# Hybrid encoder layer: q and k squared and normalised from PSUM, the softmax sum as a column of v, f16 halves for q and k

## The chip, the cores and the metric

The kernel runs on one core of one Trainium2 chip. The metric is the device time of one execution in microseconds, from the profile's first to last instruction for traces, and as measured by repeated runs for times. Lower is better. The core has five engines with a program of their own: PE (TensorE, matmul, with its weight loads shown as PEld), DVE (VectorE), ACT (ScalarE), POOL (GpSimd) and SP (SyncE, which here issues nearly all DMAs).

## The reference

Two sequences of 1024 positions and 1024 channels go through one encoder layer. What matters here is the attention half:

```python
h = rms_norm(x, norm1); proj = h @ w_in
q = rms_norm(q.reshape(B, S, N_KV, GROUP, HEAD_DIM), q_gain)   # 8 heads of 64
k = rms_norm(k.reshape(B, S, N_KV, HEAD_DIM), k_gain)          # 2 kv heads
scores = einsum(q, k of the three neighbouring blocks of 128) / sqrt(64)
scores = where(|rel| <= 128 and inside, scores + bias[bucket(rel), head], -1e30)
m = max(max(scores), sink)
e = exp(scores - m)
probs = e / (sum(e) + exp(sink - m))
out = probs @ v
```

Beside it stands a gated mixing branch (gu, gv, a 128 x 128 matrix per head). Both are normalised, concatenated, projected by w_o and added to x, and a SwiGLU FFN follows. Everything is float32 in the reference.

## The kernel before, in words

Float32 products are made of halves: every operand is split into a high and a low part (`split`, `split_gain`, L113 to L127, ACT for the high part, DVE for the rest), and a product is three matmuls, high times high, high times low, low times high (`mm3`, L224). In the attention stage the parts are f32r or, for v and the probabilities, f16. In the FFN they are f16.

The 2 x 1024 positions are 16 tiles of 128 rows. The kernel has these stages:

1. Start: x and w_q arrive by k-slices, the q products of tiles 0 to 3 run as data arrives (L246 to L258), then w_kv, the row statistics, and the bias. The bias is a row per head, `row_d` in DRAM, made by one matmul of the table with a one-hot matrix. It is loaded so that partition p holds the row shifted by p (`sh`, L290), and `bias_turn` (L294) multiplies by a reversing matrix on PE and copies the product to SBUF on DVE, eight times.
2. Attention, tile after tile, laid out by an event list. Each function is put at a time with `at(time, fn, ...)` (L562 to L639), times are `8 * t` for tile t plus offsets from the tables AT and TW (L46 to L66), and the list is sorted and emitted. These numbers are priorities and no microseconds: the tool that orders each engine's instructions moves a ready one forward where an earlier one would wait, so that the q and kv products of later tiles (`fill`) stand between the score groups of earlier ones.
3. Gating products, the output projection by seven products for two pairs of halves (a Strassen-like scheme), and the FFN in the same scheme, up to the end.

One tile of stage 2 passes through:

- `proj_pieces` (L325): 24 matmuls into a PSUM tile pq (512 columns), ACT scales them by the row's factor into SBUF `qk` (L335), then 24 matmuls into pkv (256 columns).
- `proj_evac` (L350): ACT scales k into `qk` (L353) and v's high half (L356), then squares the 640 columns of q and k into `sq` (L359).
- `qk_sum` (L361): DVE makes v's low half (L364) and the ten sums of squares (L368), and POOL raises them to the power -1/2 (L161).
- `qk_scale` (L371): DVE multiplies `qk` by the ten factors in place (L374).
- `qk_turn` (L376): PE transposes k into pk and q into pt, two PSUM tiles.
- `qk_hi` and `qk_lo` (L385, L392): ACT writes the high halves of k and q with their gains, DVE the low halves, all f32r.
- `Attn.scores` (L415), four times a tile, one call for a pair of heads (one of each kv head): six matmuls, three per head, the two heads on the upper and lower 64 rows of the array at once (L423). DVE adds the bias and takes the minimum of the negated scores in one operation with an accumulator (L428).
- `exps` (L439): ACT exponentiates with an accumulator that gives the softmax sum (L444).
- `turn` and `turn_dma` (L464, L472): the probabilities are split into f16 halves (ACT L468, DVE L469) and transposed by DMA into pT (L476).
- `pv` (L480): per head and key block three f16 matmuls of 64 columns (L489 to L491) into one PSUM tile po of all eight heads.
- `norm`, `norm2`, `finish`, `finish_pow`, `finish2` (L453 to L513): the sink's term, the reciprocal of the sums, the scaling of po (L495), its own norm, and the store.

PSUM has two pools of four banks: `mm` holds pq, pkv (from tile 4 on), pk, pt, po and the gating products; `xx` holds the scores, pkv of tiles 0 to 3 and small things. SBUF tiles of 4 KB a partition come from pools named by tag: "L" 12, "M" 8, "XL" 3, "XN" 3, "S" 9. L holds k's halves (two tiles a sequence), v's halves (one), part of pT, the outputs o, and later the gating matrices, parts of w_o, FFN operands and w_down.

Of the kernel before, what the change touches and what calls it, by code (L numbers as in the profile page):

```python
# [9 lines left out]
F32 = mybir.dt.float32  # L10
# [6 lines left out]
P = 128  # L17
# [24 lines left out]
W_NORM = 16384.0  # L42
A_NORM = 16384.0
# [3 lines left out]
    loadx=-43.881, xhi=-33.043, xlo=-30.276, rsum=-29.644, rpow=-29.313, proj=-23.505, pstep=0.544, evac=0.058, qksum=-15.892,  # L47
    scale=-12.631, turnq=-12.312, hi=-10.517, lo=-7.619, sc=0.192, tr=3.624, trd=4.116, pv=2.327, ex=2.811,
    norm=6.71, norm2=11.259, finish=17.507, finish_pow=17.97, finish2=40.676, gmf=-26.818, gmstep=2.858, ld_gv=-5.686, st1=1.728,
    ld_gu=21.124, sp_gv=-2.88, sp_gu=25.516, gvstep=0.02, gustep=0.288, bias=-3.338, biasstep=0.673, st2=11.369,  # L50
# [3 lines left out]
    mx0=-13.949, mx1=-11.679, xr0=-11.199, xr1=-7.545, ta=-5.743, tb=-3.638, tc=1.886, nu=8.268, nt=8.797, h0=10.459,  # L54
    p0=13, h1=14.83, p1=15.401, raw0=45.957, raw1=54.748, prep=52.704, preps=0.249, tl=57.369, tls=0.412, tk=58.051,
    tks=0.597, ul=64.811, uls=0.974, uk=67.481, uks=0.956,
)
TW = {
# [11 lines left out]
def kernel(  # L70
# [25 lines left out]
    slots = {"L": 12, "M": 8, "XL": 3, "XN": 3, "S": 9}  # L96
# [4 lines left out]
    def h16(name, shape=(P, KD, 512), dt=F32R):  # L101
        return big.tile(list(shape), dt, tag="h16", name=name)

# [42 lines left out]
    qgs, kgs = (cst[:, 3 * KD + 2 * NH + n : 3 * KD + 2 * NH + n + 1] for n in range(2))  # L146
    n2s = cp.tile([P, KD], F32, name="n2s")

    qg8 = cp.tile([P, 1], F32, name="qg8")
    nc.vector.tensor_scalar_mul(qg8, qgs, -1.0 / math.sqrt(HD))  # L150
# [52 lines left out]

    xms = {}

# [13 lines left out]
    def rstd1_pow(t):  # L219
        e = small("x_e", 1)  # L220
        nc.vector.tensor_scalar_add(e, xms.pop(t), EPS)
        nc.gpsimd.tensor_tensor(rstd1[t], e, nhalf[:, :1], ALU.pow)

# [22 lines left out]
    for k in range(KD):  # L246
# [16 lines left out]
        if k == 2:  # L263
            ps_row = xx("ps_row", [NH, 512])
            nc.tensor.matmul(ps_row, tabs, oh, start=True, stop=True)
            rows = k4("S", "rows", (NH, 512))
            nc.vector.tensor_scalar_mul(rows, ps_row, -1.0)
            nc.gpsimd.dma_start(row_d, rows)
# [4 lines left out]
    for t in range(GROUP):  # L273
        rstd1_load(t, "L")

    rev = k4("S", "rev", (P, P))
    nc.gpsimd.memset(rev, 0.0)
    nc.gpsimd.affine_select(
        out=rev,
        in_=rev,  # L280
        compare_op=ALU.not_equal,
        fill=1.0,
        base=1 - P,
        pattern=[[1, P]],
        channel_multiplier=1,
    )
    shifted = []
    for h in range(0, NH, 2):
        sh = k4("M", f"sh{h}", (P, 2, 384))
# [1254 lines left out]
```

## Time and profile before

| what | value |
|---|---|
| timed runs | 1838.2, 1835.81, 1833.97 us, median 1835.81 |
| profiled execution, span | 1834.5 us |
| instructions | 26027 |
| PE busy | 1809.8 us, 99% |
| DVE busy | 1161.2 us, 63% |
| ACT busy | 1005.3 us, 55% |
| POOL busy | 104.4 us, 6% |
| mean granted TensorE clock | 0.998 |

The profiled execution shows no time of its own beside its span; the timed runs are other executions of the same program. A group row of the profile reads: line, engine, operation, output <- inputs, shapes, count, then busy time in us and the mean of one in ns, then the idle time of the engine just before such instructions and what ended it. A timeline row reads: start in us, duration in us, engine, line, operation, and in brackets an idle time before it and what ended that. A row of the stretches' view reads: from and to, its length, busy time of each engine with the number of instructions, the granted TensorE clock, the busy share of the DMA engines, and GB/s. A row of waits reads: who waited, for whom, the total in us, how often, and the longest. Matmuls are pipelined, so that their durations overlap, and the distance from start to start tells the pace.

### The profile page before, as it was taken

The page shows a single profiled execution, that of the slowest core. Times are in us where ns is not written, and L with a number is a line of the kernel's source. Part 1 is how long each engine was busy: PE and PEld are TensorE (multiplying, and loading weights), DVE is VectorE, ACT ScalarE, POOL GpSimd, SP SyncE. Part 2 cuts the span into 40 slices and gives each one's busy share as a digit, 9 for nine tenths or more (in the row PEclk, how much of TensorE's full clock was granted, in tenths as well). Part 3 has the DMA queues.
Part 4 walks back from the last instruction along what each step waited for, and adds up shares of the span by engine and source line. Part 5 has one row for each costly group of instructions (what it writes and reads, how often), then busy time and mean ns, then how long its engine had stood idle before and what let it go on. Part 6 is the DMA issues. An engine that isn't in the chain of part 4 may idle for free.

```text
span 1834.5 us, 26027 instructions
## 1 busy us (share of the span) xinstructions
PE 1809.8 (99%) x9696; PEld 988.6 (54%) x9696; DVE 1161.2 (63%) x2191; ACT 1005.3 (55%) x1926; POOL 104.4 (6%) x139
## 2 busy tenths in 40 slices
PE   8999999999999999999999999999999999999999
PEld 7677767887555444444444444444444444444444
DVE  4988883657788796564564555645646946554751
ACT  6899997655677775453444534534534553333340
POOL 2212110101100000000000000000000000000000
PEclk9999999999999999999999999999999999999999
DMA  7798998433556774331322313313362754333641
GB/s 244 165 195 176 193 194 280 139 112 105 183 193 202 246 249 137 124 128 54 127 89 107 109 69 121 110 40 120 108 232 87 268 185 150 92 115 104 231 137 46
DMA packets 206427, 273.66 MB, mean 149 GB/s; under 512 B 102707, under 2 KB 129331, under 8 KB 206300
## 3 DMA queue, kind: packets, MB, share of 16 engines
q1 hardware_dynamic: 206124, 271.72, 48.2%
q8 instruction: 76, 1.25, 0.3%
q10 hardware_dynamic: 144, 0.26, 0.1%
q14 instruction: 51, 0.42, 0.1%
q0 software_dynamic: 32, 0.02, 0.0%
HBM read 172.84 MB, written 76.04 MB: 136 GB/s over the span
## 4 chain that ended last, share of the span: by engine, by line
PE 91%; DVE 3%; DMA 2%; ACT 2%; issue 1%; POOL 0%; SPq 0%; ACTq 0%; POOLq 0%; DVEq 0%
PE pd L1382 7%; PE pd L1383 7%; PE pd L1381 7%; PE pa L1119 4%; PE pa L1121 4%; PE pa L1120 4%; PE pd L1119 4%; PE pd L1121 4%; PE pd L1120 4%; PE pc L1120 4%; PE pc L1121 4%; PE pc L1119 4%; PE pb L1119 2%; PE pq L226 2%; PE pb L1120 2%; PE pb L1121 2%
## 5 line engine op out<-in xcount | busy, mean ns | idle before, releaser
L1383 PE MATMUL pd<-wop,a 128*128 128x512 f16 x616 | 233.5, 379 | 0.0
L1382 PE MATMUL pd<-wop,a 128*128 128x512 f16 x616 | 233.5, 379 | 0.0
L1381 PE MATMUL pd<-wop,a 128*128 128x512 f16 x616 | 233.5, 379 | 0.0
L1120 PEld LDWEIGHTS <-op 128*128 128x128 f16 x1232 | 120.6, 98 | 147.2 <-issue 5.4
L1119 PEld LDWEIGHTS <-op 128*128 128x128 f16 x1232 | 122.4, 99 | 142.9 <-issue 0.5
L1121 PEld LDWEIGHTS <-op 128*128 128x128 f16 x1232 | 120.7, 98 | 146.0 <-issue 1.1
L1119 PE MATMUL pa<-top,op 128*128 128x512 f16 x352 | 133.9, 380 | 2.0 <-ACT ua L1226 2.0
L1121 PE MATMUL pa<-top,op 128*128 128x512 f16 x352 | 134.1, 381 | 0.0
L1120 PE MATMUL pa<-top,op 128*128 128x512 f16 x352 | 133.9, 380 | 0.0
L126 ACT ACTIVATE wop<-wd,wdr_r 128x512 f16<-128x512 f32 x66 | 47.2, 719 | 151.6 <-PE pd L1383 149.0
L126 ACT ACTIVATE a<-as,asr_r 128x512 f16<-128x512 f32 x154 | 102.0, 709 | 33.3 <-DMA as<-act_d 13.0
L1237 ACT COPY ub<-pc 128x512 f32<-128x512 f32 x44 | 25.7, 585 | 159.6 <-PE pc L1121 159.6
L127 DVE SCALAR_TENSOR_TENSOR a<-as,asr_r,a 128x512 f16<-128x512 f32 x154 | 108.7, 745 | 6.4 <-ACT a L126 6.4
L127 DVE SCALAR_TENSOR_TENSOR wop<-wd,wdr_r,wop 128x512 f16<-128x512 f32 x66 | 49.1, 747 | 99.2 <-ACT wop L126 99.2
L1381 PEld LDWEIGHTS <-a 128*128 128x128 f16 x616 | 60.4, 98 | 72.6
L1383 PEld LDWEIGHTS <-a 128*128 128x128 f16 x616 | 60.3, 98 | 72.7
L1382 PEld LDWEIGHTS <-a 128*128 128x128 f16 x616 | 60.3, 98 | 72.6
L1061 ACT ACTIVATE junk_e<-g 128x1024 f32<-128x1024 f32 x44 | 46.4, 1053 | 69.9 <-DVE g L1216 69.9
L1243 DVE TENSOR_TENSOR ub<-ub,ua 128x512 f32<-128x512 f32 x44 | 30.4, 690 | 81.8 <-ACT ub L1237 79.4
L444 ACT ACTIVATE sc<-sc,mx 128x384 f32<-128x384 f32 (+1 forms) x128 | 74.4, 583 | 10.9 <-DVE mx L428 10.6
L1213 ACT ACTIVATE g<-g,rs 128x512 f32<-128x512 f32 x57 | 41.1, 722 | 62.4 <-DVE g L1253 35.5
L1119 PE MATMUL pc<-top_5h,op 128*128 128x512 f16 x176 | 66.7, 379 | 1.5 <-ACT ub L1237 1.5
(373 smaller groups left out, 4559.6 us busy)
## 6 DMA issues: line engine op xcount, KB each, us to landing
as<-act_d SPq DMA_DIRECT2D x77, 512.0 KB, 3.6
act_d<-g SPq DMA_DIRECT2D x66, 256.0 KB, 2.0
xs<-in_xT_dram SPq DMA_DIRECT2D x28, 512.0 KB, 4.7
raw<-in_wg_dram SPq DMA_DIRECT2D x24, 512.0 KB, 3.8
raw<-in_wu_dram SPq DMA_DIRECT2D x24, 512.0 KB, 4.3
act_d<-sa SPq DMA_DIRECT2D x44, 256.0 KB, 2.5
act_d<-sb SPq DMA_DIRECT2D x44, 256.0 KB, 2.8
wds<-in_wd_dram SPq DMA_DIRECT2D x22, 512.0 KB, 4.1
```

The lines of the kernel that those rows point to most:

```text
L126: nc.scalar.mul(hi, src, gain)
L127: nc.vector.scalar_tensor_tensor(lo, src, gain, hi, ALU.mult, ALU.subtract)
L226: nc.tensor.matmul(ps, xh, w_hi, start=first, stop=False)
L444: nc.scalar.activation(sc[:, v, :W], sc[:, v, :W], AF.Exp, bias=self.mn[:, h : h + 1], scale=-1.0, accum_out=self.sums[:, h : h + 1],)
L1061: nc.scalar.activation(junk_e[0], src, AF.Square, accum_out=acc)
L1119: nc.tensor.matmul(ps, op[:, 0, k, :], th[:, k, :], start=first and k == 0, stop=False, **more)
L1120: nc.tensor.matmul(ps, op[:, 0, k, :], tl[:, k, :], start=False, stop=False, **more)
L1121: nc.tensor.matmul(ps, op[:, 1, k, :], th[:, k, :], start=False, stop=last and k == 3, **more)
L1213: nc.scalar.activation(dst, src, AF.Silu, scale=iv)
L1381: nc.tensor.matmul(ps, a[:, 0, s, cs], wop[:, 0], start=first and n == 0, stop=False, **kw)
L1382: nc.tensor.matmul(ps, a[:, 0, s, cs], wop[:, 1], start=False, stop=False, **kw)
L1383: nc.tensor.matmul(ps, a[:, 1, s, cs], wop[:, 0], start=False, stop=end, **kw)
```

## The change

- q is no longer scaled by the row's factor from PSUM. ACT squares pq and pkv's k part straight into `sq`. The row's factor cancels in the normalisation, so the sums get an epsilon times the row's mean square (`e_all`) instead, and `qk_scale` multiplies pq and pkv from PSUM into `qk` in two DVE operations. pq and pkv thus stay in PSUM up to there; k's transpose goes into columns 256 to 383 of pkv's own bank.
- q and k halves are f16, scaled by their gains' means; a scale `qk_sc` in the score reduction (L428) and `bias_sc` in the bias row undo it. The constants come from a chain of small operations at the very start.
- The bias is not turned on PE. The one-hot rows are made in reverse order, `bias` is loaded by one DMA from `row_d`, and L428 reads it with a step of -1. `bias_turn`, `rev` and `sh` are gone.
- v's tile has 257 columns a block: kv head 0's high half, a column of ones, kv head 1's high half, and both low halves. Matmuls with a high half have 65 columns, and the softmax sum comes out in po. `exps` has no accumulator, `norm2` is gone.
- po is two PSUM tiles a tile of rows, one for each two pairs of heads, and each is finished by `half` (sum, reciprocal, product).
- Pool L has 10 tiles, and a new pool V has 2, of the size of v's tile: v of both sequences, and later the gating matrices, the last part of w_o, one FFN operand and one block of w_down.
- The tables AT and TW have new numbers.

```diff
-    slots = {"L": 12, "M": 8, "XL": 3, "XN": 3, "S": 9}
+    slots = {"L": 10, "M": 8, "XL": 3, "XN": 3, "S": 9, "V": 2}
...
+    qkc = cp.tile([P, 16], F32, name="qkc")
+    nc.vector.tensor_mul(qk2, qks, qks)
+    ps_qk = xx("ps_qk", [P, 2])
+    nc.tensor.matmul(ps_qk, onec, qk2, start=True, stop=True)
+    nc.vector.tensor_scalar_add(qkt, ps_qk, 1e-37)
+    nc.gpsimd.tensor_tensor(qkr, qkt, nhalf[:, :2], ALU.pow)
...
+    load(bias, bass.AP(tensor=row_d.tensor, offset=row_d.offset + 1, ap=[[1, P], [512, NH], [1, 384]]))
-    def bias_turn(h):
-        ps = xx(f"pj{h}", [P, 384])
-        nc.tensor.matmul(ps, rev, shifted[h // 2][:, h % 2], start=True, stop=True)
-        nc.vector.tensor_copy(bias[:, h], ps)
...
     def seq_tiles(s):
-        kT[s] = [k4("L", f"k{c}{s}", (P, TS * P), F32R) for c in "hl"]
-        vS[s] = k4("L", f"v{s}", (P, TS, 2, P), F16)
+        kT[s] = k4("L", f"k{s}", (P, 2, TS * P), F16)
+        vt = k4("V", f"v{s}", (P, TS, 4 * HD + 1), F16)
+        vS[s] = (vt[:, :, 0 : 2 * HD + 1], vt[:, :, 2 * HD + 1 :])
+        nc.gpsimd.memset(vS[s][0][:, :, HD : HD + 1], 1.0)
...
+        sq = k4("XN", f"sq{t}")
+        nc.scalar.activation(sq[:, 0:AW], pq, AF.Square)
+    def proj_evac(t):
+        nc.scalar.activation(sq[:, AW : AW + P], pkv[:, 0:P], AF.Square)
+        for v in range(NKV):
+            nc.scalar.mul(vhi(s, i, v), pkv[:, P + v * HD : P + (v + 1) * HD], rs)
...
+        ex = small("qk_x", 1)
+        nc.vector.tensor_scalar_mul(ex, e_all[:, t : t + 1], EPS * HD)
+        nc.vector.tensor_scalar(e, ss, ex, 1.0 / HD, ALU.add, ALU.mult)
...
     def qk_turn(t):
-        pk = mm(f"pk{t}", [P, P])
+        pk = pkv[:, 256 : 256 + P]
...
-                    in1=bias[:, h, self.off : self.off + W],
-                    scale=1.0,
+                    in1=backwards(bias[:, h, 384 - self.off - W : 384 - self.off]),
+                    scale=qk_sc,
...
-                    accum_out=self.sums[:, h : h + 1],
...
+                self.po[c] = mm(f"po{self.t}_{c}", [P, 2, NKV, HD + 1])
+                vh = vS[self.s][0][:, i, v * HD : v * HD + HD + 1]
+                nc.tensor.matmul(po, pT[:, 0, bs], vh, start=b == 0, stop=False)
+                nc.tensor.matmul(po[:, v : v + HD], pT[:, 0, bs], vlo(self.s, i, v), start=False, stop=False)
+                nc.tensor.matmul(po, pT[:, 1, bs], vh, start=False, stop=b == self.nb - 1)
...
+            nc.vector.tensor_add(e, po.rearrange("p j v d -> p j (v d)")[:, :, HD : HD + 2], e)
+            nc.vector.reciprocal(f, e)
...
-    ws_hi = k4("L", "ws_hi", (P, NH, P), F32R)
+    ws_hi = k4("V", "ws_hi", (P, NH, P), F32R)
```

The new AT moves, among others, evac from 0.058 to 0.005, turnq from -12.312 to -12.649, hi from -10.517 to -10.207, pv from 2.327 to 2.095, ex from 2.811 to 2.525, st2 from 11.369 to 13.229, and adds half0 at 13.0.

More of the change, by code (lines that the diff above doesn't have):

```diff
@@ L202, in split_x @@
         split_x_lo(t)
+    done = set()
     xms = {}
+    e_all = cp.tile([P, NT], F32, name="e_all")
     xns = {}
@@ L423, in scores @@
                     nc.tensor.matmul(
-                        ps[v][:, :W], qT[t][rows, a, hp, :], kT[self.s][b][rows, keys], start=n == 0, stop=n == 2
+                        ps[v][:, :W], qT[t][rows, a, hp, :], kT[self.s][rows, b, keys], start=n == 0, stop=n == 2
                     )
@@ L501, in finish @@
+        def finish(self):
+            self.half(1)
+            o = self.o
             self.ms = small("a_ms", 1)
@@ L579, in xlo @@
         split_x_lo(t % NT)
-    for n in range(NH):
-        at(AT["bias"] + n * AT["biasstep"], bias_turn, n % 2 * GROUP + n // 2)
     for t in range(NT):
```

203 lines of the change are left out of this document (108 added, 95 removed), and 15 rows, old and new, of the table TW.

## The prediction

> **What bounds the kernel now.** First the head of the page, then busy time by stretch, then TensorE's waits.
>
> ```profile
> span 1834.5 us, 26027 instructions
> 17.00:60.00 43.00, 39.28 (x227) 31.34 (x226) 26.18 (x73) 28.35 (x62) 11.88 (x11) 1.00 0.53 182
> 57.00:250.00 193.00, 190.73 (x1858) 148.63 (x1858) 167.04 (x474) 181.74 (x440) 37.56 (x36) 1.00 0.93 194
> 252.00:284.00 32.00, 27.01 (x281) 19.67 (x278) 21.77 (x62) 27.00 (x64) 2.77 (x3) 0.98 1.02 206
> PE ps L423 <- DVE mx L428: 0.7, 2, 0.5
> PE po L489 <- DMA pT<-ph: 1.1, 1, 1.1
> ```
>
> The change lies in the attention stage, up to about 284 us. The columns after the length are PE, PEld, DVE, ACT and POOL busy time, then the granted clock, the DMA share and GB/s. From 57 to 250 us PE is busy for 190.7 of 193 us at full clock; the two wait rows, from that same stretch, are the largest there, 1.8 us. PE bounds it, with ACT (181.7, 94%), the DMA engines (93%) and DVE (167.0, 87%) close behind. A busy PE is no proof of a full one, so I read starts of neighbouring matmuls. From 252 to 284 us PE loses 5 us and the DMA share is full: there the transposes of the probabilities set the pace. The rest of the 1834.5 us is FFN and projections, which the change reaches only through buffers.
>
> **Scores as f16 halves (the main term).** The timeline of one steady group, the pace of both types elsewhere, and the weight loads:
>
> ```profile
> 129.01 0.28 PE L227 MATMUL pkv<-wkv,xh 128*128 128x256 f32 x1
> 129.13 0.28 PE L228 MATMUL pkv<-wkv,xl 128*128 128x256 f32 x1
> 129.34 0.44 PE L423 MATMUL ps<-kh,qt 64*128 64x384 f32 x2
> 129.62 0.34 PE L423 MATMUL ps<-kl,qt 64*128 64x384 f32 x2
> 129.80 0.34 PE L423 MATMUL ps<-kh,qt 64*128 64x384 f32 x2
> 130.07 0.20 PE L489 MATMUL po<-v,pT 128*128 128x64 f16 x1
> 130.11 0.19 PE L490 MATMUL po<-v,pT 128*128 128x64 f16 x1
> 130.14 0.19 PE L491 MATMUL po<-v,pT 128*128 128x64 f16 x1
> 28.10 0.39 PE L226 MATMUL pq<-wq_hi,xh_s 128*128 128x512 f32 x1
> 28.33 0.39 PE L227 MATMUL pq<-wq_lo,xh_s 128*128 128x512 f32 x1
> 450.53 0.38 PE L905 MATMUL wa<-wo0h,mo 128*128 128x512 f16 x1
> 450.74 0.38 PE L906 MATMUL wa<-wo0l,mo 128*128 128x512 f16 x1
> L423 PEld LDWEIGHTS ps<-kh,qt x256: 182/183/188, 52.6 to 268.2; 64*128 64x128 f32 x128
> L490 PEld LDWEIGHTS <-pT x352: 96/98/133, 63.6 to 283.5; 128*128 128x128 f16 x176
> 57.00:250.00 193.00, 43.30 (x326) 26.14 (x326) 1.00 0.93 194
> ```
>
> A group is three pairs, each pair on two halves of the array. The first pair takes 0.28 us to the next start, the second 0.18; its duration, 0.44 against 0.34, says why: 0.10 us of it is the wait for its own weights, 183 ns in f32. In f16 a load is 98 ns, so I take 0.09 off. The pace per 512 columns falls from 0.23 to 0.21 us, for 384 about 0.013 a pair, three times: 0.04. Together **0.13 us a group**. The last row, of L423's instructions alone, counts 326 matmuls between 57 and 250 us, six a group: 54 groups, **7.0 us**. Bounds: 0.04 a group (2.2 us) if the 0.10 us is not the load, and 0.18 (9.7 us) if the entry, 0.21 us after L228 where its neighbours take 0.12, shrinks by half as well. Groups before and after this stretch wait for others; I count them at nothing.
>
> The entry speaks to a rule. The Trainium skill, "TensorEngine Tiling (Array Packing)", section Key Properties, says that changing the tiling mode drains the engine. If the first pair's 0.10 us is that drain rather than the load, f16 leaves it there and the sum keeps only the lower bound.
>
> **Start-up without the bias turns.**
>
> ```profile
> 42.56 1.46 PE L296 MATMUL pj<-sh,rev 128*128 128x384 f32 x4
> 43.85 0.27 PE L379 MATMUL pk<-ident,qk 128*128 128x128 f32 x1
> 48.10 1.56 PE L296 MATMUL pj<-sh,rev 128*128 128x384 f32 x4 [2.35 <-DVE v L364]
> 52.62 0.38 PE L423 MATMUL ps<-kh,qt 64*128 64x256 f32 x1
> 36.51 1.97 POOL L161 TENSOR_TENSOR qk_r<-qk_e,nhalf 128x10 f32<-128x10 f32 x1 [4.58 <-DVE qk_e L159]
> L297 DVE COPY bias<-pj 128x384 f32<-128x384 f32 x8 | 4.2, 545 | 0.0
> L374 DVE TENSOR_TENSOR qk<-qk,qk_r 128x640 f32<-128x640 f32 x16 | 13.2, 824 | 12.1 <-POOL qk_r L161 12.1
> L495 DVE TENSOR_TENSOR o<-po,f 128x512 f32<-128x512 f32 x16 | 10.9, 682 | 4.9 <-PE po L491 4.9
> L364 DVE SCALAR_TENSOR_TENSOR v<-pkv,rs,v 128x128 f16<-128x128 f32 x16 | 5.5, 345 | 2.1 <-ACT v L356 2.1
> ```
>
> Between 42.56 us and the first scores at 52.62, PE gives two turns 1.29 us (42.56 to 43.85), so the eight cost 5.2, but it also waits, 2.35 us in one piece: the pace is DVE's and POOL's, square sum, power (1.97 us), scaling, tile after tile. So the eight copies count, 545 ns less some 0.08 of overlap: 3.7 us. The change adds to DVE per tile one more half of v (two of 64 columns for one of 128, about +0.13 by L364), a scaling split into 512 and 128 from PSUM (682 + 345 less overlap against 824, +0.10) and one small operation (0.08): 0.3 a tile, 0.9 for three. Net **-3 us**. Bounds: nothing, if the power chain alone sets it, and -7, if the turns and the wait both go. What is late next is that chain; the reversed load replaces four loads of the same bytes and lands long before. The chain of gains at the very start (nine small operations, a matmul and a power before the first split) has the first input's wait as its cover; without it, +0.8 us; I take 0.
>
> **Costs that lie beside PE.**
>
> ```profile
> L444 ACT ACTIVATION_READ_ACCUMULATOR sc<-sc,mx 128x1 f32 x128 | 24.2, 189 | 0.0
> L359 ACT ACTIVATE sq<-qk 128x640 f32<-128x640 f32 x16 | 11.8, 737 | 0.0
> L428 DVE CUSTOM_DVE_ANT_0 sc<-ps,bias 128x384 f32<-128x384 f32 x96 | 49.5, 549 | 4.4 <-PE ps L423 4.4
> L462 DVE RECIPROCAL f<-ab 128x8 f32<-128x8 f32 x16 | 3.1, 196 | 0.1
> ```
>
> ACT loses eight accumulator reads a tile (about 0.1 each beyond their overlap) and the 640-wide square (0.64), and gains one more piece of v (0.16): -1.3 us of some 13.4. DVE gains the 0.3 above, a second sum and reciprocal (0.2) and a split final product (0.08): +0.6 of 12.4. ACT falls to 88%, DVE rises to 94% of a shorter stretch. Both stay under PE, so nothing on the path; the cover is DVE's remaining 6%. Two unknowns hang on it. Bias read with a step of -1 keeps its 549 ns by my choice, the only row of that operation; from a few per cent shorter to doubled (0.4 x 8 = 3.2 us a tile, and DVE would bind) is its range. And 65 columns instead of 64, from f16 addresses that are odd for half the blocks: 0.03 us a matmul now (130.11 to 130.14), one column is 0.4 ns, for 704 matmuls **+0.3 us**; at worst the odd half, 528, doubles: +16 us. It can't gain, since columns are added.
>
> **Buffers.**
>
> ```profile
> L115 DVE TENSOR_TENSOR ws_lo<-ws_st,ws_hi x1: 1215/1215/1215, 284.5 to 284.5; 128x1024 fp32r<-128x1024 f32 x1
> L685 PE MATMUL sg<-vh,ws_lo x32: 274/282/284, 323.3 to 457.0; 128*128 128x256 f32 x32
> L905 PE MATMUL wd<-wo6h,mo x32: 379/379/379, 470.9 to 621.6; 128*128 128x512 f16 x32
> ```
>
> ws_lo now takes v's second slot, free after the last PV, about where it runs already, and is read 38 us later. wo6 must wait for the last gating matmul at 457.0 and is read at 470.9; four ACT and four DVE pieces fit. I take 0, at most +1.
>
> **Sum.** 1834.5 - 7.0 - 3 + 0.3 = 1824.8 for the span. The three timed runs have a median of 1835.81, 1.3 above the span, so **1826**.
>
> **Rivals.**
>
> ```profile
> 125.56 0.67 ACT L335 ACTIVATE qk<-pq,rstd_all 128x512 f32<-128x512 f32 x1
> 135.82 0.83 DVE L374 TENSOR_TENSOR qk<-qk,qk_r 128x640 f32<-128x640 f32 x1 [0.54 <-POOL qk_r L161]
> 252.68 19.50 SPq L476 DMA_TRANSPOSE pT<-ph  x9
> ```
>
> (1) **Transposes take PE's place.** Nine back to back need 19.5 us, 2.2 each, four a tile, beside the loads and a store; the DMA share is 0.93. Then the 7 us are lost and only the start-up counts: 1834.5 - 3 + 1.3 = 1833. Against it: PE waits 1.1 us for them up to 250 us.
>
> (2) **PSUM: slower.** pq's bank was free when L335 had copied it, at 125.6 us; now it is held until the scaling, at L374's place 136.6, 11 us more in a tile of 14.3 (193 us for 54 groups, four a tile). pkv is held past the transposes, about as long again. Only pk's own bank (5 us) goes, and po's two shorter holds save some 2. By the events' numbers the four mm banks were held for 3.0 on average and now for 3.7. Each tile's first q matmul can then stop PE, and every fill queued behind it, the scores among them, until DVE has scaled. It decides from 10 us / 13 tiles = 0.8 us a tile; at 1.7 a tile, one DVE subtraction and one scaling late, 22 us come back: about 1848. For it: DVE at 94%. Against it: 3.7 of four leaves some slack, and fills can be issued early, while a bank is free.
>
> (3) **f16 does not shorten the entry** (the lower bound): 1834.5 - 2.2 - 3 + 0.3 + 1.3 = 1831.
>
> **How the numbers follow.** The forecast has 0.60 (1816 to 1830 by its bounds), rival 1 0.14, rival 2 0.15, rival 3 0.11. Within 0.2%, about what a measurement of this kernel can tell from no change, is 1832.1 to 1839.5. Faster: forecast and rival 3, 0.71; same: rival 1, 0.14; slower: rival 2, 0.15. The range reaches down to both best bounds (9.7 + 7, and a little of the 5 us that PE loses at the end), 1814, and up past rival 1 into the milder half of rival 2 and of the odd-address cost, 1841.
>
> **What would show it.** Right: L423's successor with the first pair at about 0.19 us to the next start and loads near 98 ns; first scores at 49 to 50 us; PE busy from there to the weights of the gating; attention's last PV near 273. Wrong: PE waits in the waits view on DVE's scaling (rival 2) or on pT before 250 us (rival 1); the score reduction over 549 ns; PV matmuls over 0.03 us apart for every other block; a first pair still at 0.28 (rival 3).

## The result, and the profile after

The changed kernel takes 1845.69 us (median of 4 runs, 1844.99 to 1846.03) against 1835.44 us for the kernel before (4 runs, 1833.97 to 1838.2): a ratio of 1.006, 95% interval 1.0048 to 1.0071. It is 0.6% slower, where 0.5% faster was forecast. The profiled execution has a span of 1843.2 us. Each trace, here and below, is of one execution; spans lie from 4.7 us below to 1.6 above their kernel's median. So traces are read for the place of a loss, and ratios for its size.

The same three stretches as before, by windows (the last one made longer, since attention ends later), with PE, PEld, DVE, ACT and POOL busy time, granted clock, DMA share and GB/s:

```profile
17.00:60.00 43.00, 36.15 (x203) 28.93 (x202) 24.74 (x80) 27.13 (x59) 12.26 (x12) 0.84 0.54 188
57.00:250.00 193.00, 184.84 (x1746) 135.08 (x1747) 166.43 (x501) 152.16 (x305) 38.80 (x33) 0.97 0.84 181
252.00:296.00 44.00, 39.30 (x408) 26.37 (x408) 38.18 (x113) 40.42 (x76) 5.18 (x5) 0.96 1.09 241
```

Between 57 and 250 us PE is busy for 184.8 us instead of 190.7, and it gets 1746 matmuls done instead of 1858. ACT fell to 79%, in the direction forecast. DVE's busy time in this stretch did not rise (166.4 after 167.0 us), but the stretch holds fewer tiles: in the nine middle tiles, which are counted below, DVE is busy for 13.4 us a tile, after 12.1 before. The waits of PE in that stretch:

```profile
PE po L516 <- DVE qk L384: 5.8, 7, 2.0
PE pkv L253 <- DVE k L418: 0.8, 1, 0.8
PE po L516 <- DVE o L531: 0.7, 2, 0.4
```

The largest is new: the first PV matmul of a group (L516) needs an mm bank, and the bank comes free when DVE has scaled q out of it (L384). One such stop, DVE first, then PE:

```profile
130.25 0.66 DVE L384 TENSOR_TENSOR qk<-pq,qk_r 128x512 f32<-128x512 f32 x1
131.05 0.19 PE L516 MATMUL po<-v,pT 128*128 128x65 f16 x1 [1.04 <-DVE qk L384]
131.08 0.19 PE L517 MATMUL po<-v,pT 128*128 128x64 f16 x1
131.11 0.19 PE L518 MATMUL po<-v,pT 128*128 128x65 f16 x1
```

PV reads nothing that L384 writes, so this is a wait for the bank. That is rival 2 by name. The start shows something that no part of the prediction had:

```profile
42.06 0.60 PE L404 MATMUL pt<-ident,qk 128*128 128x128 f32 x4
46.80 0.87 PE L404 MATMUL pt<-ident,qk 128*128 128x128 f32 x3 [4.14 <-DVE qk L384]
...
48.34 0.37 PE L450 MATMUL ps<-k,qt 64*128 64x256 f16 x1 [0.24 <-ACT k L410]
```

```profile
48.00:54.00 6.00, 3.98 (x20) 2.39 (x20) 3.00 (x11) 3.05 (x6) 1.99 (x3) 0.50 0.01 3
54.00:60.00 6.00, 5.31 (x19) 2.52 (x16) 5.20 (x15) 5.62 (x11) 0.00 (x0) 0.50 0.34 90
60.00:66.00 6.00, 6.00 (x18) 2.03 (x18) 3.73 (x11) 2.91 (x6) 0.00 (x0) 0.50 0.65 129
66.00:72.00 6.00, 6.00 (x41) 4.47 (x39) 3.34 (x8) 1.79 (x4) 0.00 (x0) 0.65 0.88 235
```

The first scores start at 48.34, 4.3 us earlier than before. But ahead of them PE stands idle for 4.14 us, and from 48 to 66 us the granted clock is 0.50, where it was 1.00 in the kernel before.

A measure of progress that all kernels below share is DVE's score reduction, 128 of them, eight a tile. In this kernel's timeline tile 3 starts with the first of these rows and tile 12 with the second:

```profile
94.78 0.62 DVE L455 CUSTOM_DVE_ANT_0 sc<-ps,bias,qkc 128x384 f32<-128x384 f32 x1 [0.34 <-DMA pT<-ph]
...
231.24 0.60 DVE L455 CUSTOM_DVE_ANT_0 sc<-ps,bias,qkc 128x384 f32<-128x384 f32 x1
```

Nine tiles lie between, 15.16 us each. By this measure the time goes as follows (the run with f16 halves and the reversed bias alone is one of the experiments):

| us | before | f16 and bias alone | after |
|---|---|---|---|
| to tile 3 | 89.45 | 91.73 | 94.78 |
| tile 3 to tile 12 | 129.87 | 126.66 | 136.46 |
| a tile | 14.43 | 14.07 | 15.16 |
| tile 12 to the last reduction | 49.63 | 49.24 | 51.84 |
| from there to the end of the span | 1565.6 | 1560.8 | 1560.1 |

So 5.3 us are lost up to tile 3, 6.6 in the middle, 2.2 behind it, and 5.4 come back after attention. Those 5.4 are in part chance: behind the last reduction the profiled execution of the kernel before has the clock at 0.50 twice, for 3.41 us each (from 282.78 and from 671.90 us), and the other two have it at 1.00. In the twenty traces this last stretch takes 1558.5 to 1562.1 us where the clock stays up and 1561.7 to 1569.5 where it falls. Against the kernel with the two good parts alone the middle is the main loss: 9.8 us of 14.8.

### The profile page after: what moved, and what is told of

The parts are those of the page before. It is cut to its first block, busy times and chain, and to the rows that moved or that the text cites. A ratio compares the mean times of both kernels' runs of the same rounds, so it can differ in the third digit from the quotient of the medians.

```text
span 1843.2 us, 25958 instructions
## 1 busy us (share of the span) xinstructions
PE 1808.9 (98%) x9682; PEld 977.8 (53%) x9682; DVE 1175.9 (64%) x2288; ACT 985.2 (53%) x1798; POOL 109.0 (6%) x139
## 4 chain that ended last, share of the span: by engine, by line
PE 85%; DVE 6%; ACT 3%; DMA 3%; issue 2%; POOL 0%; SPq 0%; ACTq 0%; DVEq 0%; POOLq 0%
PE pd L1424 7%; PE pd L1422 7%; PE pd L1423 7%; PE pd L1160 4%; PE pa L1160 4%; PE pc L1160 4%; PE pa L1162 4%; PE pd L1161 4%; PE pa L1161 4%; PE pc L1162 4%; PE pc L1161 4%; PE pd L1162 4%; PE pb L1160 2%; PE pb L1161 2%; PE pb L1162 2%; DMA pT<-ph 2%
## 5 line engine op out<-in xcount | busy, mean ns | idle before, releaser
L472 ACT ACTIVATE sc<-sc,mx 128x384 f32<-128x384 f32 (+1 forms) x128 | 70.2, 585 | 11.9 <-DVE mx L455 11.5
L455 DVE CUSTOM_DVE_ANT_0 sc<-ps,bias,qkc 128x384 f32<-128x384 f32 (+1 forms) x128 | 70.0, 577 | 6.0 <-PE ps L450 5.3
```

What stands on the lines that cost most here:

```text
L455: nc.vector.tensor_tensor_reduce(out=sc[:, v, :W], in0=ps[v][:, :W], in1=backwards(bias[:, h, 384 - self.off - W : 384 - self.off]), scale ...
L472: nc.scalar.activation(sc[:, v, :W], sc[:, v, :W], AF.Exp, bias=self.mn[:, h : h + 1], scale=-1.0,)
```

## The experiments

Theory A is the clock: the gap at the start halves it, and that is the loss. Theory B is the banks: q and kv stay in PSUM until DVE has scaled them, and PE waits for a bank. Theory C is DVE's queue: the added operations make DVE late, and PE waits for it. A fourth candidate came up on the way, the order that the event times make. Ratios are against the kernel before, measured on the same chip; 0.1% is 1.8 us.

**f16 halves alone**, on the kernel before:

```
-        kT[s] = [k4("L", f"k{c}{s}", (P, TS * P), F32R) for c in "hl"]
+        kT[s] = [k4("L", f"k{c}{s}", (P, TS * P), F16) for c in "hl"]
-        qT[t] = k4("S", f"qt{t}", (P, 2, NH // 2, P), F32R)
+        qT[t] = k4("S", f"qt{t}", (P, 2, NH // 2, P), F16)
```

> The kernel before with q's and k's halves in f16 and nothing else. By the prediction's first step a score group is 0.13 us shorter, 54 times: 7 us, so about 1828, with PE still free of waits up to 250 us. Rival: the transposes or DVE take PE's place as the pace and most of it is lost: 1833 to 1836, with new waits of PE on pT or mx.

Measured: 1828.21 us, ratio 0.997 (0.9958 to 0.9982), 5.5 us by the ratio and 6.7 by the medians; 14.01 us a tile. One group in PE's timeline, and the weight loads:

```profile
127.81 0.28 PE L228 MATMUL pkv<-wkv,xl 128*128 128x256 f32 x1
128.03 0.34 PE L423 MATMUL ps<-kh,qt 64*128 64x384 f16 x2
128.20 0.33 PE L423 MATMUL ps<-kl,qt 64*128 64x384 f16 x2
128.36 0.33 PE L423 MATMUL ps<-kh,qt 64*128 64x384 f16 x2
128.62 0.20 PE L489 MATMUL po<-v,pT 128*128 128x64 f16 x1
```

```profile
L423 PEld LDWEIGHTS <-qt 64*128 64x128 f16 x384 | 14.5, 94 | 23.4 <-issue 16.7 <-DVE mx L428 0.7 <-ACT xn L217 0.5
```

The first pair takes 0.17 us to the next start (0.28 before), its duration is 0.34 like the others', a load 94 ns, and the group 0.59 us instead of 0.73. The 0.10 us went away with the f32 load, so it was the wait for the weights and no drain. The entry, the pair's start 0.22 us after its predecessor, is as it was; what it consists of is not shown. **The first step of the prediction stands.**

**The reversed bias alone**, on the kernel before (its table of buckets is not turned, so the bias values are mirrored; the work is that of the change):

```
-    for n in range(NH):
-        at(AT["bias"] + n * AT["biasstep"], bias_turn, n % 2 * GROUP + n // 2)
+    load(bias, bass.AP(tensor=row_d.tensor, offset=row_d.offset + 1, ap=[[1, P], [512, NH], [1, 384]]))
-                    in1=bias[:, h, self.off : self.off + W],
+                    in1=backwards(bias[:, h, 384 - self.off - W : 384 - self.off]),
```

> The kernel before with the bias loaded once in reverse and read with a step of -1, so without the eight turns; scale stays a constant. Theory A: PE then has a gap of over 3 us around 44 to 52 us, the granted clock falls there, and although the first scores come some 4 us sooner the end comes later: about 1840. Rival: the turns were only in the way: clock 1.00, about 1831. Beside that: if the step of -1 costs what the changed kernel's reduction shows, the 384-column one takes 610 ns; if it is the scale from a pointer that costs, it stays at 549.

Measured: 1833.21 us, ratio 0.9992 (0.9984 to 1.0). Its reduction and its clock:

```profile
L412 DVE CUSTOM_DVE_ANT_0 sc<-ps,bias 128x384 f32<-128x384 f32 x96 | 49.6, 551 | 9.3 <-PE ps L407 9.3
```

```profile
48.00:54.00 6.00, 4.56 (x20) 2.92 (x20) 4.84 (x15) 2.65 (x7) 1.95 (x1) 0.50 0.01 3
54.00:60.00 6.00, 5.87 (x21) 3.74 (x22) 5.94 (x19) 6.00 (x18) 0.79 (x2) 0.50 0.56 135
```

Two answers. The step of -1 is free (551 ns after 549), so the changed kernel's 610 ns is the scale from a pointer. And taking the turns away alone opens the gap and halves the clock, yet this kernel is not slower: theory A's price is too high.

**Theory A directly.** Twenty products of 128 columns, which nothing reads, behind the first tile's transposes of the changed kernel:

```
+    at(-13.98 + AT["st2"], lambda: [nc.tensor.matmul(live[3][1][:, 384:512], ident, onec, start=True, stop=True) for _ in range(20)])
```

> The changed kernel with twenty extra 128-column products behind the first tile's transposes, into columns of pkv3's bank that nothing reads. Theory A: PE's idle 4.14 us at 42.66 let the granted clock fall to 0.50 from 48 to 66 us, and the matmuls at half pace there cost some 9 us. Then PE is busy up to about 46.9 us, the clock stays near 1.00 from 48 to 72, the last PV comes near 286 instead of 294.9 and the time is about 1836. Rival B: the scalings from PSUM and a fuller DVE set the pace in any case; then the clock is restored but the waits on L384 grow by what it gives, and the time stays at 1843 to 1846.

Measured: 1845.52 us, ratio 1.0061 (1.0048 to 1.0074). PE's timeline, and the windows:

```profile
45.23 4.99 PE L676 MATMUL pkv<-onec,ident 128*128 128x128 f32 x28 [2.51 <-DVE v L368]
```

```profile
48.00:54.00 6.00, 5.70 (x39) 4.85 (x39) 2.21 (x7) 2.19 (x4) 2.06 (x3) 0.84 0.00 0
54.00:60.00 6.00, 4.52 (x27) 2.36 (x26) 5.61 (x18) 5.65 (x11) 0.00 (x0) 1.00 0.10 31
60.00:66.00 6.00, 6.00 (x38) 3.38 (x39) 5.85 (x19) 4.86 (x10) 0.00 (x0) 1.00 1.00 208
```

The products began 2.51 us late, behind DVE's reading of their bank, but the clock is at 1.00 from 54 us on. Tile 3 starts at 90.41 instead of 94.78, so the low clock is worth 4.4 us there, and tile 12 at 227.16 instead of 231.24. At the last reduction 1.7 of them are left, and the timed runs show no gain. A tile still takes 15.19 us: **the low clock at the start is real and is not the loss.**

The same question without added work: tile 4's row factor is added up by GpSimd, and the last start tile's square sum is set later, so that DVE's 2.63 us wait for `e_all` no longer stands ahead of the second scaling.

```
-        nc.vector.tensor_scalar_add(e, xms.pop(t), EPS)
+        (nc.gpsimd if t == GROUP else nc.vector).tensor_scalar_add(e, xms.pop(t), EPS)
...
-            at(-16.0 + t + AT["st1"], qk_sum, t)
+            at(-16.0 + t + AT["st1"] if t < 3 else 0.0, qk_sum, t)
```

> The changed kernel with the sum of tile 4's rstd taken from DVE to GpSimd and the third tile's square sum set later, so that DVE's 2.63 us wait for e_all no longer stands ahead of the second tile's scaling. No work is added. Theory A: PE's idle falls from 4.14 to under 3 us; if that is short enough, the clock stays at 1.00 and the time is about 1835; if it is not, the clock still falls and the time is 1843 to 1845. Rival B: 1844 whatever the clock does, with the waits on L384 as they were.

Measured: 1841.65 us, ratio 1.0041 (1.0029 to 1.0053). The gap shrank to 2.93 us and the clock fell all the same (0.59 and 0.50 from 48 to 66 us); tile 3 comes at 92.10, a tile takes 15.28 us. DVE's blocked queue at the start was worth some 3.5 us; what a clock at 1.00 would have given was not tested by it.

**Undoing one step of the change.** The scale as a constant:

```
-                    scale=qk_sc,
+                    scale=1.0 / QK_SC,
```

> The changed kernel with the reduction's scale as a constant, 1/128, in place of the pointer to qk_sc; where the gains' product calls for another scale the result would differ. The reduction should go back from 610 to about 549 ns, eight times a tile: 0.5 us of DVE. Theory C (DVE is too full, and its late scaling holds PE): a tile falls from 15.16 to some 14.7 us and the time to 1838 to 1841. Theory B (the banks are held too long whatever DVE does): 1843 to 1845.

Measured: 1853.38 us, ratio 1.0102 (1.0088 to 1.0115); a tile takes 15.53 us. The reduction is back at 552 ns, DVE has 0.47 us less to do in a tile, and the kernel is slower by 0.4% than the change. Neither theory had that. The timelines say how it can be: the instructions of PE, DVE and ACT stand in another order, with the same event times. The next three moved the order as well, so this way of undoing measures the step and a new order together.

q and k copied out of PSUM by ACT again, scaled in SBUF, k's transpose in its own bank:

```
-        sq = k4("XN", f"sq{t}")
-        nc.scalar.activation(sq[:, 0:AW], pq, AF.Square)
+        qk = k4("S", f"qk{t}")
+        nc.scalar.copy(qk[:, 0:AW].rearrange("p (j v d) -> p v j d", v=NKV, d=HD), pq.rearrange("p (v j d) -> p v j d", v=NKV, d=HD))
...
-        pk = pkv[:, 256 : 256 + P]
+        pk = mm(f"pk{t}", [P, P])
```

> The changed kernel with q and k copied out of PSUM by ACT again, scaled in SBUF in one operation, and k's transpose in a bank of its own: the step 'straight from PSUM' undone, the rest kept. Theory B: PE's waits on the scaling (5.1 us between 90 and 232 us) go, a tile falls from 15.16 towards 14.2 us, and the time is 1834 to 1838. Theory C: ACT takes 0.95 us more a tile and DVE nothing less; the time stays at 1843 to 1847.

Measured: 1845.35 us, ratio 1.0057 (1.0044 to 1.007). PE's waits from 57 to 250 us:

```profile
PE po L508 <- DMA pT<-ph: 4.6, 1, 4.6
PE pk L393 <- DVE qk L387: 4.3, 6, 1.4
```

A tile takes 14.97 us, tile 12 starts 7.4 us earlier than in the change (223.84), and tiles 12 and 13 give it back (at 263.04 tile 14 starts, 263.82 in the change). The waits for a bank that L384 had held are gone, as theory B expects, but others stand in their place: here PE waits for the transposes of the probabilities, and at the transposition of k (L393) for the scaling of k that it reads.

The sums by ACT's accumulators and one output bank a tile:

```
-                self.po[c] = mm(f"po{self.t}_{c}", [P, 2, NKV, HD + 1])
+                self.po = mm(f"po{self.t}", [P, NH, HD])
...
+                    accum_out=self.sums[:, h : h + 1],
```

> The changed kernel with the softmax sums taken by ACT's accumulators again, PV in 64 columns and one bank of output a tile: the step 'ones column' undone, v's layout kept. Theory C: DVE loses some 0.3 us a tile (the second sum, reciprocal and product), ACT gains 0.75: 1841 to 1844. Theory B: one output bank held for the whole tile instead of two for half of it leaves fewer banks to the projections: 1846 to 1852. If 65 columns cost PE time: some 3 us less than either.

Measured: 1855.55 us, ratio 1.0113 (1.0096 to 1.013), 15.87 us a tile; PE waits 9.8 us for `o`, the output's release. With q held in PSUM, one output bank a tile is dearer than two half banks, as theory B expects, and by more than its 1846 to 1852.

The event times of before:

```
-    loadx=-44.85, xhi=-31.606, xlo=-29.381, rsum=-29.644, rpow=-27.887, proj=-23.448, pstep=0.534, evac=0.005,
+    half0=13.0, loadx=-43.881, xhi=-33.043, xlo=-30.276, rsum=-29.644, rpow=-29.313, proj=-23.505, pstep=0.544, evac=0.058,
...
```

> The changed kernel with the event times of the kernel before (half0 stays at 13). If the new times are what costs, 1835 to 1840; if the new times belong to the new steps, slower than 1846, up to 1852; if the order matters little, 1844 to 1847. It also tells whether PE's order 'PV, then scores' (before: scores, then PV) comes from the times.

Measured: 1849.75 us, ratio 1.008 (1.0066 to 1.0093), 15.23 us a tile. The new times fit the new steps better, by about 4 us. PE's order is 'scores, then PV' here and 'PV, then scores' with the new times.

**The event times by themselves**, on the kernel before (three entries that the change no longer has stay):

```
-    loadx=-43.881, xhi=-33.043, xlo=-30.276, rsum=-29.644, rpow=-29.313, proj=-23.505, pstep=0.544, evac=0.058, qksum=-15.892,
+    bias=-3.338, biasstep=0.673, norm2=11.259, loadx=-44.85, xhi=-31.606, xlo=-29.381, rsum=-29.644, rpow=-27.887,
...
```

> The kernel before with the event times of the change and no other edit: what setting the events anew does by itself to a kernel whose work is the same. If the order of the instructions is worth several us by itself, 1840 to 1850, with PE waits that were not there; if PE's cover hides it, 1834 to 1837.

Measured: 1845.61 us, ratio 1.0064 (1.0051 to 1.0077). The same work in another order costs as much as the whole change did. Tile 3 starts 6.1 us later, a tile takes 14.56 us instead of 14.43, and the stretch from tile 12 to the last reduction 5.3 us more. So no step can be priced by a run that changes the order. The build-up keeps the event times of before throughout; with them PE's order hardly moves, but DVE's and ACT's still do.

**Building up from below**, with the event times of before. The base is the changed kernel with the four edits above together (constant scale, q and k copied out, sums by ACT, old times). Each of the next three leaves one of them away:

```
base:     scale=1.0 / QK_SC,   nc.scalar.copy(qk, pq),          accum_out=self.sums
psum:     scale=1.0 / QK_SC,   nc.scalar.activation(sq, pq),    accum_out=self.sums
ones:     scale=1.0 / QK_SC,   nc.scalar.copy(qk, pq),          half(0), half(1)
pointer:  scale=qk_sc,         nc.scalar.copy(qk, pq),          accum_out=self.sums
```

> Built up from the other side, with the event times of before: the changed kernel with q and k copied out by ACT and scaled in SBUF, the sums by ACT's accumulators, and a constant scale; so only f16 halves, the reversed bias and the slots of the change are left. If f16 (-6.7 us measured alone) and the bias (-1.7 alone) add, 1826 and a tile of 14.0 us. If the slots or the start-up with its low clock cost, 1830 or more.

Measured: 1834.01 us, ratio 1.0005 (0.9996 to 1.0014), 14.57 us a tile. From 57 to 250 us PE waits 5.3 us at the transposition of k, which no kernel with 14.0 us a tile does for more than 0.7. Straight from PSUM:

> The same with q and k squared and scaled straight from PSUM. Theory B (banks held until DVE's scaling): new waits of PE on the scaling, a tile of some 14.8 us, and 6 to 12 us more than the run without. Rival: DVE's share alone decides; this step adds only 0.2 us of DVE a tile, so at most 2 us more.

Measured: 1855.23 us, ratio 1.0116 (1.0102 to 1.013), 1.1% more than its base; 16.17 us a tile. Its waits from 57 to 250 us:

```profile
PE po L520 <- DVE o L526: 10.9, 6, 2.7
PE pkv L400 <- DVE qk L389: 4.2, 4, 1.5
```

The first row is a wait for a bank: a tile's first PV needs the one that the scaling of an earlier output (L526) frees. The second is a wait for an operand: the transposition of k reads what L389 has scaled. Theory B named such waits, at 6 to 12 us; the price is nearly twice that.

The ones column with its half banks:

> The same base with the ones column in v, the two half banks of output and the sums from PSUM. If 65 columns and the two halves cost nothing on PE, within 2 us of the base; theory C: DVE gains 0.35 us a tile, up to 3 us more; theory B: the output's banks are held for less time each, so at or below the base.

Measured: 1844.01 us, ratio 1.0062 (1.0049 to 1.0074), 0.57% more; 15.45 us a tile, with 6.2 us of waits for the bank of the transposes, pt, on DVE's product `o` (L522). No theory had named this size. DVE now has two releases of output banks a tile to make instead of one; that this is the reason is only argued. The pointer:

> The same base with the reduction's scale from the pointer: 61 ns more, eight times a tile, 0.5 us of DVE. Theory C: DVE goes from some 12.2 to 12.7 us a tile and a tile lengthens by 0.2 to 0.5 us, 3 to 7 us in all. Rival: PE still covers it, within 1.5 us of the base.

Measured: 1836.74 us, ratio 1.0013 (1.0005 to 1.0022), 0.08% more, with intervals that overlap; 14.85 us a tile. So half a microsecond more of DVE a tile costs nothing here that is clear of noise, and theory C's 3 to 7 us did not come.

The base is no faster than before, so the two good parts were run without the change's slots, gain chain and split v, by the first two diffs of this section in one kernel, with the table turned:

```
-    rel = np.arange(512) - 255
+    rel = 256 - np.arange(512)
```

> The kernel before with f16 halves and the bias loaded in reverse and read backwards, nothing else (the bucket table turned as in the change, v's layout, slots and sums as before). If the two gains measured alone add, 1834 - 6.7 - 1.7 = 1826. If the low clock after the missing turns, or a busier DVE, takes back what f16 gives, 1830 to 1834, like the base run, which has the change's slots, gain chain and split v besides.

Measured: 1830.63 us, ratio 0.9986 (0.9977 to 0.9995); 14.07 us a tile. The two gains don't add: 0.3% and 0.08% alone, 0.14% together, though the intervals of f16 alone and of both overlap. And with twenty products to keep PE fed:

```
+    at(-13.98 + AT["st2"], lambda: [nc.tensor.matmul(live[-4][:, 384:512], ident, onec, start=True, stop=True) for _ in range(20)])
```

> The run before this one with twenty 128-column products that nothing reads, placed by the schedule among the transposes of the first tiles. Theory A for this kernel: the clock stays at 1.00 and 3 to 5 us are won, about 1822. Rival, as the same edit did to the changed kernel: the clock is back, the tiles run earlier, and the wait for transposes and for DVE behind them takes it: no change.

Measured: 1832.37 us, ratio 0.999 (0.9981 to 1.0). Tile 3 comes 1.6 us earlier (90.10), the last reduction 2.2 us earlier (265.39), the first gating matmul at 319.0 instead of 319.2: what the clock costs there is waited away between the last PV and the gating. Theory A has fallen twice.

**Bank and queue apart.** On this last base (f16 and bias, without the extra products) PE's order hardly moves with the following edits. DVE's and ACT's orders do move, so DVE's time and DVE's order are not parted. One more DVE operation a tile (the first line), and then two (both):

```
+        nc.vector.tensor_tensor(sq[:, 640:1024], sq[:, 0:384], sq[:, 128:512], ALU.mult)
+        nc.vector.tensor_tensor(sq[:, 640:1024], sq[:, 0:384], sq[:, 256:640], ALU.mult)
```

> The kernel before with f16 halves and the reversed bias (1830.6), and one more DVE operation a tile, 384 columns into columns that nothing reads, some 0.45 us: what the pointer and the split pieces add to DVE, without any other edit. PE's order is all but the same as without it. Theory C (a fuller DVE is late, and PE waits for it): 3 to 6 us more, tiles of 14.3 to 14.6 us. Theory B (it is the banks): within 1.5 us.

> As the run with one more DVE operation a tile, with two of them: some 0.9 us of DVE, a share of about 0.93 if a tile kept its 14.07 us. Theory C: 6 to 12 us more than without them. If DVE has the slack that its share suggests: within 2 us.

And q left in its bank until DVE scales it:

```
-        nc.scalar.mul(
-            qk[:, 0:AW].rearrange("p (j v d) -> p v j d", v=NKV, d=HD),
+        nc.scalar.activation(sq[:, 0:AW].rearrange("p (j v d) -> p v j d", v=NKV, d=HD), pq.rearrange("p (v j d) -> p v j d", v=NKV, d=HD), AF.Square)
...
+        nc.vector.tensor_tensor(
+            qk[:, 0:AW].rearrange("p (j v d) -> p v j d", v=NKV, d=HD),
+            pq.rearrange("p (v j d) -> p v j d", v=NKV, d=HD),
...
```

> The same base with the one edit that q stays in its bank until DVE scales it from there (ACT only squares it); k, v, the sums and the outputs are as before, and eps is added to the unscaled squares. DVE gains 0.15 us a tile, ACT loses some 0.6. PE's order is all but the same. Theory B: PE waits on the scaling for banks, a tile of 15 us or more, 8 to 20 us in all. Theory C: within 2 us.

| kernel | us | ratio | us a tile | DVE busy a tile | scaling late by |
|---|---|---|---|---|---|
| base: f16 and bias | 1830.63 | 0.9986 (0.9977 to 0.9995) | 14.07 | 12.24 | 0.20 |
| one DVE operation more (0.55 us) | 1838.47 | 1.0023 (1.0015 to 1.0031) | 14.77 | 12.63 | 1.02 |
| two of them (1.10 us) | 1841.26 | 1.0038 (1.0025 to 1.005) | 14.88 | 13.01 | 1.28 |
| q held in its bank | 1851.35 | 1.0089 (1.0074 to 1.0104) | 16.29 | 12.34 | 1.16 |

The last column is the mean time, in tiles 4 to 11, from the end of POOL's power to the start of DVE's scaling of q and k, which waits for that power.

Waits of PE from 57 to 250 us with one operation more:

```profile
PE po L474 <- DMA pT<-ph: 2.2, 3, 1.7
PE pk L364 <- DVE ab L446: 2.2, 3, 1.0
PE pkv L230 <- DVE kl L381: 2.0, 2, 1.8
PE pk L364 <- DVE f L447: 1.8, 3, 0.7
```

With q held, the waits, the stretch, and one tile's square and scaling:

```profile
PE pk L369 <- DVE qk L364: 11.0, 6, 4.5
PE pk L369 <- DVE ab L451: 6.1, 4, 3.9
```

```profile
57.00:250.00 193.00, 175.88 (x1699) 127.59 (x1698) 151.12 (x438) 158.97 (x399) 34.05 (x32) 0.96 0.82 172
```

```profile
66.70 0.59 ACT L321 ACTIVATE sq<-pq 128x512 f32<-128x512 f32 x1
...
78.75 0.68 DVE L357 TENSOR_TENSOR qk<-pq,qk_r 128x512 f32<-128x512 f32 x1
```

In the last run pq is out for some 12 us longer, yet its rows show no wait for a bank. L369 is the first transposition of a tile, which reads the k that L364 has just scaled. Here is the stop of 3.9 us, in the order POOL, DVE, DVE, PE:

```profile
141.36 1.96 POOL L165 TENSOR_TENSOR qk_r<-qk_e,nhalf 128x10 f32<-128x10 f32 x1 [13.90 <-DVE qk_e L163]
145.84 0.69 DVE L357 TENSOR_TENSOR qk<-pq,qk_r 128x512 f32<-128x512 f32 x1
146.44 0.28 DVE L364 TENSOR_TENSOR qk<-qk,qk_r 128x128 f32<-128x128 f32 x1
146.87 0.45 PE L369 MATMUL pk<-ident,qk 128*128 128x128 f32 x1 [3.90 <-DVE ab L451]
```

The profile names `ab`, but in this run every stop of over 0.4 us between 57 and 250 us, nine with 16.8 us together, stands at L369 and ends 0.14 or 0.15 us after the end of L364. PE waits for an operand. The stops at L364 in the run with one operation more are of the same kind: they end 0.14 or 0.15 us after the scaling (L359). A tile of the base and one of that run:

```profile
91.97 1.96 POOL L165 TENSOR_TENSOR qk_r<-qk_e,nhalf 128x10 f32<-128x10 f32 x1 [9.53 <-DVE qk_e L163]
93.97 0.83 DVE L358 TENSOR_TENSOR qk<-qk,qk_r 128x640 f32<-128x640 f32 x1 [0.46 <-POOL qk_r L165]
```

```profile
88.07 2.54 POOL L165 TENSOR_TENSOR qk_r<-qk_e,nhalf 128x10 f32<-128x10 f32 x1 [8.64 <-DVE qk_e L163]
92.29 0.82 DVE L359 TENSOR_TENSOR qk<-qk,qk_r 128x640 f32<-128x640 f32 x1
93.25 0.30 PE L364 MATMUL pk<-ident,qk 128*128 128x128 f32 x1 [0.73 <-DVE f L447]
```

In the base DVE stands ready and scales 0.04 us after the power has ended. With one operation more the power itself is longer, and the scaling starts 1.68 us after it, because DVE has other work ahead of it in its order: the rest of a subtraction for `ph`, two reductions and small things. That is theory C in kind, and the tile grows with this lateness more than with DVE's busy time. The second operation adds as much to DVE as the first, but only 0.11 us to the tile and 0.15% to the time, where the first added 0.70 us and 0.37%. (Up to 0.2 us of the 0.70 are a clock of 0.50 for 3.41 us, which the other run does not have.) The base of the build-up and the run with the pointer fit in: their scalings are 0.76 and 0.97 us late, their tiles 14.57 and 14.85 us. Why DVE's order came out so is not followed, and no run moves the scaling alone. So a held bank has no price from these runs: the 1.0% of the last one is that of the whole edit, two scalings and a new order of DVE and ACT with it. A stop has a second effect there: the two longest (3.9 and 4.5 us) are followed by a clock of 0.50, which is up to 0.8 us of that run's 2.2 us a tile.

What happens in the changed kernel is seen in the nine middle tiles, first of the change, then of the base with f16 and bias:

```profile
94.78:231.24 136.46, 130.06 (x1299) 97.92 (x1298) 120.59 (x372) 110.55 (x224) 33.35 (x29) 1.00 0.87 185
```

```profile
91.73:218.39 126.66, 126.42 (x1295) 93.80 (x1294) 110.12 (x317) 120.85 (x297) 27.88 (x27) 1.00 0.96 195
```

The same matmuls, at full clock: PE idles for 6.4 us instead of 0.2, and is busy for 3.6 us more. Of the 6.4 us, 5.8 are waits for a bank that DVE frees: 5.1 for the scaling of q (L384), 0.7 for the output (L531). So here, other than in the run with q held, the bank is what PE stops for. DVE has 10.5 us more to do, ACT 10.3 less: the change moves work from ACT, which had little on PE's path, to DVE, which frees PE's banks and scales its operands. Part of the 3.6 us is order: PE's timeline has 42 entries into scores for the 36 groups, since PV cuts into some (after four or three of their six matmuls), where the base has 36 for 36. The rest was not followed further.

## Why the prediction was wrong

- *Scores as f16 halves, 7.0 us.* Right in mechanism and size: 0.14 us a group measured (0.13 forecast), 5.5 to 6.7 us alone. Rival 3 fell: the first pair's 0.10 us went with the f32 load. With it fell the reading that these 0.10 us are the drain at a change of tiling mode that the Trainium skill, "TensorEngine Tiling (Array Packing)", Key Properties, tells of; whether the unchanged entry holds such a drain, no run here shows.
- *Start-up, net -3 us.* The first scores came 4.3 us earlier, a little more than forecast. But "what is late next is that chain" missed what the turns had also done: they kept PE fed. Without them PE idles for 3.54 us (bias alone) to 4.14 us (the change), the clock halves, and up to tile 3 nothing is left of the gain in these two. The bias edit alone is worth 0 to 2.9 us by its interval.
- ***Costs that lie beside PE, taken at nothing: the step that failed.*** It said that ACT at 88% and DVE at 94% "both stay under PE, so nothing on the path; the cover is DVE's remaining 6%". A share is no cover. In the nine middle tiles PE idles for 6.4 us instead of 0.2, nearly all of it for banks that DVE frees late, with DVE at 88%. What PE needs from DVE is a bank or an operand at a certain time, and that depends on what stands ahead of it in DVE's order. The size was wrong as well: DVE gained 1.2 us a tile on the base with the two good parts, where 0.6 was forecast. Some 0.5 of it is the scale from a pointer, 61 ns eight times a tile, which the prediction did not see. Of its two unknowns, the step of -1 is free as chosen, and the 65 columns too (within a group PV's matmuls stay 0.03 us apart).
- *Rival 2, 0.15.* Its mechanism is in the trace: q's bank is held some 10 us longer (11 forecast), and PE waits on L384. Its price of 22 us is neither borne out nor refuted. Squaring and scaling from PSUM cost 1.1%, some 20 us, on the base of the build-up, but there waits for operands stand beside those for banks. "It decides from 0.8 us a tile" was near: the changed kernel loses 1.1 us a tile against the two good parts. "3.7 of four leaves some slack", a mean from the events' numbers, was no argument against it: PE does stop for a bank. Undoing the two half banks of the output (1855) or the new event times (1850) makes the changed kernel slower still; both also move the order.
- *Rival 1.* No: PE's waits for pT up to 250 us did not grow to PE's place.
- *Buffers, at most +1.* Not tested alone. The base with slots, gain chain and split v is 0.2% slower than the one without them, with a later scaling.
- *The bounds of the forecast.* Those of its terms give 1819 to 1834 (1835.8 + 0.3, less 16.7 or 2.2), not 1816 to 1830. The result lies outside of either.
- *Missing from it:* that the order of the instructions is part of the change. Setting the event times anew moves the old kernel by 0.64%.

What stays open: the single prices don't add up to the change's 0.6%, and undoing one step of the change alone never gave the time back, because each edit also reorders. So it is seen what PE waits for in the changed kernel, but not how its loss divides among a held bank, a late scaling and the order. Open is also how the 0.57% of the ones column divides between its two banks and DVE's added operations, and where the gain of the bias goes beside f16. A fifth bank for the projections was not tried, nor the same DVE work with the scaling put first.

The fastest kernel measured is the one before with f16 halves alone, 1828.21 us, 0.3% faster than before and 0.9% faster than the change.

## What to carry to other kernels

Before work is moved from one engine to another, ask which of the two hands something to the bound engine, a bank that comes free or an operand, and what will stand ahead of it in that engine's order. DVE at 87% had time to spare and still came too late with the scaling, while ACT at 94% had cost PE hardly a wait. When a wait appears, look whether the waiting instruction reads what the named one writes: only if it does not is it a wait for a buffer. And where a schedule is set by priorities, price each edit at a fixed order of every engine: here the order alone moved the same work by as much as all edits together.

## What was not expected of the hardware

- TensorE's granted clock falls to 0.50 in steps of 3.41 us. Between 20 and 1820 us the twenty traces have 54 stretches at 0.50. Each lasts a whole number of such steps, and in one trace all begin on one grid of 3.41 us, which lies elsewhere in the next. So it seems to count how an idle gap falls on the grid, which no run tests by itself: 0.50 followed 26 of 27 gaps of over 3 us, 16 of 28 gaps between 2.0 and 3.0, and 9 of 31 between 1.5 and 2.0. The Trainium skill, "TensorE: Matmul & The Clock Gate", Part 1, gives one idle window of about 3.4 us; the trace agrees for the length of a step and for the long gaps, and for the short ones the measurement decides.
- How long it stays low is not read from PE's busy time. With the twenty products back to back behind the gap it was at 1.00 again after 3.41 us (at 49.96 us); in the changed kernel, where score groups alternate with single projections, it stayed at 0.50 for 23.89 us (46.34 to 70.24), though PE has no pause from 60 to 66 us.
- POOL's power of ten columns takes 1.96 us in most tiles, and 2.53 to 2.61 us where DVE is in a subtraction for `ph` as it starts (tiles 6 to 9 of the changed kernel, tiles 4 to 9 with one operation more). Spans on POOL are rough, but DVE's scaling waits for it.
- The reduction with its scale from a pointer takes 610 ns for 384 columns and 477 for 256, against 549 and 418 with a constant: 59 to 61 ns whatever the width.
